# A decoder trunk on one core: the engine that adds the pool projection, and the steps at which four activation sets are fetched

## The chip, the core and the metric

The kernel runs on one core of a Trainium2 chip. A core has five engines that run their own queues of instructions in order: TensorE (PE, matmul, with its weight loads shown as PEld), VectorE (DVE), ScalarE (ACT), GpSimd (POOL) and SyncE (SP), which here issues nearly all DMAs. Engines wait for each other through semaphores. Matmuls write to PSUM banks; everything else lives in SBUF, and the large activations go through device memory between stages.

The metric is the device time of one execution in microseconds.

## What is computed

One layer of a decoder trunk over 2048 positions of width 1024, in float32, cut here to what matters:

```python
u = x * (1 + scale) + shift                      # scale, shift, gate from SiLU(c) @ w_ada
q, k, v, a_gate, p_in, p_gate, m_a, m_p = split(u @ w_in)
a = sliding_window_attention(q, k, v, sinks, bias) * silu(a_gate)
a = a @ w_attn_proj
p = einsum(causal_pool(p_in), w_pool_mix)
p = (p * pool_scale) * silu(p_gate)
p = p @ w_pool_proj
y = sigmoid(m_a) * a + sigmoid(m_p) * p          # the sum that the change touches
y = (y @ w_out) * (1 + gate)
x = layer_norm(ALPHA * x + y)
```

## The kernel before

The 2048 positions are worked in two halves s of 1024, each half in two columns t of 512. Each projection takes two products of matrices into one: a "quad" holds two blocks of 128 output rows (mi = 0, 1) for both columns, and computes its four results with seven products instead of eight, from sums and differences of the weights and of the activations (a scheme of Strassen's kind). The seven products are named B11, T1, T2, B21, T3, B22, T4 after their activation operand. Float32 precision comes from splitting each operand in a rounded part and a remainder, so one product is 4 pieces x 3 = 12 matmuls of 128 x 512.

**The sets.** The seven activation operands of a stage are tiles of their own (`set_B11`, `set_T1`, ...), each of two halves. All quads of a stage use the same seven. At a change of stage, each is fetched from device memory as raw float32 (one DMA of 512 KB for each half, on SP), cast to the rounded part on ScalarE, and its remainder is taken on VectorE (`split` in `set_steps`). A set can be fetched only when the last product of the old stage that reads it is done. Six stages take new sets in this way: the input projections of the second half, then, in the last third of the kernel, attention projection and pool projection of the first half, the same of the second half, and the output projection.

**The order of products.** `ring` runs groups of two quads. A group is 14 steps of one product each: `back` runs T2, B21 of the first quad, T2, B21 of the second (steps 0 to 3), T3, B22, T3, B22 (4 to 7), T4, T4 (8, 9), and then `front` starts the next group with B11, T1, B11, T1 (10 to 13). At the last group of a stage, `front` already belongs to the next stage, and its steps 14 to 27 are the first group of that. `tick` is called behind each product, and runs what is hooked to that step; `defer(n, f)` runs f n steps later. `PLAN` and `SPLIT_AT` name the order and the steps of the casts (B21 at 11 and 12, T3 at 13 and 14, B22 at 15 and 16, T4 at 17 and 18), `FETCH_AT` the steps of the fetches. B21 is first read at step 15, T3 at 18, B22 at 19, T4 at 22.

**The weights.** Each quad loads its weights in three DMAs (L261 to L263; from the sum y, in the output stage, L257). GpSimd makes the sums and differences of them: L268 (`sum1`, needed for T1), L272 and L273 (`mid`), L277 (`late`). ScalarE casts pairs of weight blocks (L305; L312 for the last block) into `w_set`, VectorE takes the remainders (L131). `ask` in `back` has the next quad's weights loaded one step after the current quad's third pair was split, and `sum1` two steps after that.

**Side work.** GpSimd also makes the sums of the next stages' sets: four subtractions on `spare` tiles for each eighth, stored by SP.

**The pool projection.** `pool_quad` takes each of a quad's four results as it is done: VectorE multiplies it by its gate (L610), GpSimd adds it to the attention's share in the `wide` tile (L612), and SP stores the sum to `y_d` three steps later. There are 32 such results, 16 in each half. What a helper (`split_set`, `product`, functions that record their instruction through `Ordered`) issues is shown under L56.

Of the kernel before, what the change touches and what calls it, by code (L numbers as in the profile page):

```python
# [15 lines left out]
ALU = mybir.AluOpType  # L16
# [43 lines left out]
def kernel(  # L60
# [22 lines left out]
    nc = tc.nc  # L83
# [354 lines left out]
    def defer(ticks, f):  # L438
        due.append((now[0] + ticks, len(due), f))
# [48 lines left out]

    SPLIT_AT = (2, 3, 4, 5, 6, 7, 11, 12, 13, 14, 15, 16, 17, 18)

    FETCH_AT = {"B11": -2, "T1": -1, "T2": 3, "B21": 4, "T3": 7, "B22": 8, "T4": 10}

    def set_steps(ph, store):

# [6 lines left out]
        def fetch(name, half):  # L501
            sp.dma_start(raw(name, half), store[name][half])

        def split(name, half):
            t = sets[name][:, 2 * half : 2 * half + 2]
            act.copy(t[:, :, 0, :], raw(name, half))
            low(dve, t[:, :, 1, :], raw(name, half), t[:, :, 0, :])

        for at, (_, name, half) in zip(SPLIT_AT, PLAN):
            todo.append((FETCH_AT[name], lambda n=name, h=half: fetch(n, h)))  # L510
            todo.append((at, lambda n=name, h=half: split(n, h)))
# [70 lines left out]
    def gates_ahead(name, s, m, raw):  # L582
        g = {}

        def ahead(ph, turn):
            for mi, t in (((0, 0), (1, 1)), ((0, 1), (1, 0)))[turn]:
                x = g[mi, t] = ph.c("g")
                sp.dma_start(x, gates_d[name][s, m + mi, t])
                if raw:
                    nc.scalar.activation(x, x, AF.Sigmoid)  # L590

        return g, ahead
# [12 lines left out]
    def pool_quad(s, m):  # L605
        gates, ahead = gates_ahead("mp", s, m, m < 4)

        def consume(ph, mi, t, src):
            g = gates.pop((mi, t))
            nc.vector.tensor_tensor(g, src, g, ALU.mult)  # L610
            dst = ta[m + mi][:, t * CH : (t + 1) * CH]
            nc.gpsimd.tensor_tensor(dst, g, dst, ALU.add)  # L612
            defer(3, lambda: sp.dma_start(y_d[s, m + mi, t], dst))

        return Quad((wpp[m], wpp[m + 1]), consume, ahead)
# [942 lines left out]
```

## Time and profile before

| | us |
|---|---|
| runs, median of 3 (lowest to highest) | 1728.08 (1727.62 to 1729.83) |
| the profiled execution | 1731.03 |
| its span | 1729.2 |
| TensorE busy | 1664.1 |
| VectorE busy | 1254.5 |
| GpSimd busy | 1058.1 |
| ScalarE busy | 964.2 |

The mean clock granted to TensorE in the profiled execution is 0.989 of the full one. By HBM traffic, 227.96 MB are read and 110.33 MB written.

How to read the rows further down. In a timeline: start in us from the span's start, duration in us, engine, source line, operation, output and inputs by the program's names, count; in brackets the idle time of the engine just before, and what ended it. In a list of waits: who waited for whom, total us, times, longest us. In a list of groups: line, engine, operation, shapes, count, then busy us, mean ns, and the idle time before them with its releasers. In a list of DMAs: tiles, queue, kind, count, size, median us from issue to landing. SPq is SyncE's queue.

### The profile page before, as it was taken

What the parts mean: (1) busy time and instruction counts of PE and PEld (TensorE: products, weight loads), DVE (VectorE), ACT (ScalarE), POOL (GpSimd) and SP (SyncE); (2) the same over time, 40 slices, a digit from 0 to 9 for tenths busy, and PEclk for the clock granted to TensorE, in tenths of its full rate; (3) what the DMA queues carried; (4) which work ended last, traced back from release to release, by engine and by line L of the source; (5) the groups of instructions that cost most, each with busy time, mean ns of one, the idle gap of its engine ahead of it and who ended that gap; (6) DMA issues with size and microseconds to landing.
All of it is one profiled execution on the core that took longest, in us unless ns stands there. A gap on an engine that the chain in (4) does not pass through costs nothing.

```text
span 1729.2 us, 24722 instructions
## 1 busy us (share of the span) xinstructions
PE 1664.1 (96%) x8056; PEld 1392.5 (81%) x8056; DVE 1254.5 (73%) x2256; ACT 964.2 (56%) x2002; POOL 1058.1 (61%) x782
## 2 busy tenths in 40 slices
PE   6899999999999999999999999999999989999996
PEld 5788888888888788887788888888787767787885
DVE  5966665787778768557578777786778576868877
ACT  4544446667667655334667676765644345434452
POOL 2054427686867837763476778594657875666442
PEclk9999999999999999999999999999999989999999
DMA  9388753333432377866533434235987887787442
GB/s 353 131 283 287 218 188 111 117 108 122 149 107 95 129 250 277 282 226 207 188 110 104 132 118 153 86 116 185 326 294 275 310 305 272 263 274 239 158 139 105
DMA packets 188849, 336.79 MB, mean 195 GB/s; under 512 B 18336, under 2 KB 44080, under 8 KB 188720
## 3 DMA queue, kind: packets, MB, share of 16 engines
q1 hardware_dynamic: 185600, 330.96, 55.7%
q10 hardware_dynamic: 3088, 4.23, 1.0%
q8 instruction: 64, 1.05, 0.3%
q14 instruction: 65, 0.53, 0.1%
q0 software_dynamic: 32, 0.02, 0.0%
HBM read 227.96 MB, written 110.33 MB: 196 GB/s over the span
## 4 chain that ended last, share of the span: by engine, by line
PE 47%; POOL 7%; DVE 5%; DMA 4%; issue 4%; ACT 1%; SPq 0%; POOLq 0%; DVEq 0%; ACTq 0%
PE mm L56 30%; PE lg L56 13%; PE pv L56 2%; PE pt L56 2%; DVE w_set L131 1%; POOL spare L56 1%; POOL nxt L56 1%; POOL W L268 1%; POOL w_set L56 1%; POOL fin L56 1%; DMA W<-in_wpp_dram 1%; DMA W<-in_wap_dram 1%; DMA pin_T<-spare 1%; POOL wide L612 1%; DVE set_T L56 1%
## 5 line engine op out<-in xcount | busy, mean ns | idle before, releaser
L56 PE MATMUL mm<-set_B,w_set 128*128 128x512 f32 x2664 | 664.8, 397 | 18.3 <-ACT w_set L305 10.5
L56 PEld LDWEIGHTS mm<-set_B,w_set 128*128 128x128 f32 x2664 | 501.2, 190 | 129.1 <-ACT w_set L305 12.6
L56 PE MATMUL mm<-set_T,w_set 128*128 128x512 f32 x1824 | 457.4, 397 | 3.8 <-DVE mm L56 1.2
L56 PE MATMUL lg<-set_T,w_set 128*128 128x512 f32 x1728 | 417.9, 392 | 10.0 <-DVE w_set L131 4.8
L56 PEld LDWEIGHTS mm<-set_T,w_set 128*128 128x128 f32 x1824 | 337.7, 189 | 76.4 <-DVE mm L56 4.1
L56 PEld LDWEIGHTS lg<-set_T,w_set 128*128 128x128 f32 x1728 | 323.9, 189 | 82.7 <-DVE w_set L131 8.4
L131 DVE TENSOR_TENSOR w_set<-W,w_set 128x1024 fp32r<-128x1024 f32 x138 | 198.4, 1439 | 185.9 <-ACT w_set L305 172.8
L305 ACT CAST w_set<-W 128x1024 fp32r<-128x1024 f32 x138 | 144.8, 1050 | 291.0 <-PE mm L56 164.4
L56 POOL TENSOR_TENSOR w_set<-W,w_set 128x512 fp32r<-128x512 f32 x132 | 172.0, 1311 | 102.5 <-ACT w_set L56 98.1
L268 POOL TENSOR_TENSOR W<-W,A 128x512 f32<-128x512 f32 x46 | 70.6, 1535 | 223.8 <-DVE set_T L56 58.2
L56 ACT ACTIVATE L<-L,nm 128x257 f32<-128x257 f32 (+1 forms) x256 | 127.1, 498 | 26.0 <-DVE nm L56 20.2
L56 POOL TENSOR_TENSOR W<-W 128x512 f32<-128x512 f32 x82 | 108.3, 1335 | 51.1 <-DVE sm L56 30.3
L277 POOL TENSOR_TENSOR W<-W 128x512 f32<-128x512 f32 x46 | 72.8, 1583 | 101.6 <-DVE w_set L131 94.0
L56 DVE CUSTOM_DVE_ANT_0 L<-lg,bt,nsink 128x256 f32<-128x256 f32 (+1 forms) x256 | 111.6, 473 | 19.0 <-DMA bt<-e_rep 9.1
L56 POOL TENSOR_TENSOR spare<-spare 128x512 f32<-128x512 f32 x68 | 117.2, 1725 | 12.6 <-DMA spare<-ain_B 8.7
L56 ACT CAST w_set<-W 128x512 fp32r<-128x512 f32 (+1 forms) x164 | 100.0, 626 | 37.4 <-POOL W L56 25.8
L56 DVE COPY o<-pv 64x256 f32<-64x256 f32 x128 | 54.3, 424 | 82.7 <-PE pv L56 81.4
L56 ACT CAST pth<-pt 128x512 fp32r<-128x512 f32 (+1 forms) x128 | 72.8, 569 | 62.8 <-PE pt L56 62.4
L56 ACT ACTIVATE L<-L,sm 128x256 f32<-128x256 f32 (+1 forms) x128 | 64.3, 502 | 67.9 <-DVE sm L56 67.7
L272 POOL TENSOR_TENSOR W<-W 128x512 f32<-128x512 f32 x44 | 75.6, 1720 | 39.1 <-DVE w_set L131 30.1
L273 POOL TENSOR_TENSOR W<-W 128x512 f32<-128x512 f32 x44 | 77.5, 1761 | 28.3 <-DMA W<-in_win_dram 26.6
L56 DVE TENSOR_SCALAR L<-L,sm 128x256 f32<-128x256 f32 (+1 forms) x128 | 89.8, 701 | 0.0
(225 smaller groups left out, 2474.8 us busy)
## 6 DMA issues: line engine op xcount, KB each, us to landing
W<-in_win_dram SPq DMA_DIRECT2D x42, 512.0 KB, 5.5
W<-in_win_dram SPq DMA_DIRECT2D x42, 256.0 KB, 3.7
A<-in_win_dram SPq DMA_DIRECT2D x42, 256.0 KB, 4.7
ag_d<-sig SPq DMA_DIRECT2D x32, 256.0 KB, 5.3
pg_d<-sig SPq DMA_DIRECT2D x32, 256.0 KB, 4.4
pg<-pg_d SPq DMA_DIRECT2D x32, 256.0 KB, 3.3
pin_B<-fin SPq DMA_DIRECT2D x32, 256.0 KB, 2.2
ag<-ag_d SPq DMA_DIRECT2D x32, 256.0 KB, 2.9
```

Source lines behind the costliest of these rows:

```text
L56: return lambda *args, **kw: self.tc.keep_in_program_order(op(*args, **kw))
L131: engine.tensor_tensor(dst, src, as32(hi), ALU.subtract)
L268: e.tensor_tensor(self.w[:, 1, :], self.w[:, 2, :], self.a22, ALU.add)
L272: e.tensor_tensor(x[:, 1, :], x[:, 1, :], x[:, 0, :], ALU.subtract)
L273: e.tensor_tensor(x[:, 2, :], x[:, 0, :], x[:, 2, :], ALU.subtract)
L277: e.tensor_tensor(x[:, 3, :], x[:, 3, :], x[:, 1, :], ALU.subtract)
L305: a.copy(by_two(hi), raw)
L612: nc.gpsimd.tensor_tensor(dst, g, dst, ALU.add)
```

## The change

```diff
-    FETCH_AT = {"B11": -2, "T1": -1, "T2": 3, "B21": 4, "T3": 7, "B22": 8, "T4": 10}
+    FETCH_AT = {"B11": -2, "T1": -1, "T2": 3, "B21": 8, "T3": 10, "B22": 12, "T4": 13}
...
             nc.vector.tensor_tensor(g, src, g, ALU.mult)
             dst = ta[m + mi][:, t * CH : (t + 1) * CH]
-            nc.gpsimd.tensor_tensor(dst, g, dst, ALU.add)
+            nc.vector.tensor_tensor(dst, g, dst, ALU.add)
             defer(3, lambda: sp.dma_start(y_d[s, m + mi, t], dst))
```

Two edits. The fetches of B21, T3, B22 and T4 are put into the program 4, 3, 4 and 3 products later, at each of the six changes of stage; the steps of their casts stay. In the pool projection, the 32 additions to the attention's share run on VectorE, behind the multiplication, instead of on GpSimd. Part of the instructions keep the order in which they are written; the others are placed by a scheduler, so that both edits also change which instruction stands where in the queues of VectorE, ScalarE, GpSimd and SP. TensorE's order stays.

## The prediction

> **What bounds the kernel now.** I read the page first: TensorE is busy 96% of the span.
>
> ```profile
> PE 1664.1 (96%) x8056; PEld 1392.5 (81%) x8056; DVE 1254.5 (73%) x2256; ACT 964.2 (56%) x2002; POOL 1058.1 (61%) x782
> ```
>
> So time can only go where TensorE stands still or runs at less than its full clock. The busy time by stage shows where that is; columns are window, length, busy time of PE, PEld, DVE, ACT, POOL, granted clock, DMA share, GB/s. The windows hold the openings of stages, where seven activation sets are replaced: the second half's projections, then both halves' attention and pool projections, then the output. I call them O0 to O5 (the 1413 row is no opening).
>
> ```profile
> 620.00:700.00 80.00, 80.00 (x355) 66.24 (x354) 58.85 (x50) 43.00 (x57) 47.28 (x28) 1.00 0.85 292
> 1214.00:1240.00 26.00, 23.93 (x97) 19.04 (x96) 15.71 (x13) 15.42 (x21) 17.73 (x10) 0.93 0.90 324
> 1285.00:1323.00 38.00, 36.65 (x160) 29.51 (x159) 32.52 (x29) 24.61 (x35) 24.28 (x14) 1.00 0.98 373
> 1361.00:1413.00 52.00, 42.21 (x161) 31.90 (x161) 35.77 (x32) 22.51 (x26) 41.29 (x25) 0.90 1.00 369
> 1413.00:1475.00 62.00, 60.47 (x267) 49.72 (x266) 47.13 (x43) 31.09 (x42) 36.87 (x23) 1.00 0.75 264
> 1475.00:1495.00 20.00, 17.95 (x71) 14.07 (x70) 13.89 (x12) 9.87 (x13) 15.17 (x9) 0.91 0.88 325
> 1551.00:1589.00 38.00, 35.09 (x146) 27.77 (x145) 35.17 (x30) 15.80 (x18) 28.72 (x16) 0.96 0.75 263
> ```
>
> Idle plus lost clock is 2.1 + 1.8 (0.07 of 26) at O1, 1.35 at O2, 9.8 + 4.0 at O3 (0.10 of 52 is 5.2; part of the slow clock fell on idle time), 1.5 in the 1413 window, 2.05 + 1.8 at O4, 2.9 + 1.5 at O5: 28.8 us. More than that, from these stages, no version of the change can give. O0 has none.
>
> The waits of TensorE from 1214 to 1590 say what ended the idle time: always a weight operand (w_set), its rounded part from ScalarE or its remainder from VectorE.
>
> ```profile
> PE mm L56 <- ACT w_set L305: 10.5, 5, 5.4
> PE mm L56 <- DVE w_set L131: 5.9, 6, 2.0
> PE lg L56 <- DVE w_set L131: 2.8, 4, 1.1
> PE lg L56 <- ACT w_set L305: 0.8, 1, 0.8
> ```
>
> Behind ScalarE stands GpSimd. The timeline at O3:
>
> ```profile
> 1385.67 2.19 POOL L612 TENSOR_TENSOR wide<-g,wide 128x512 f32<-128x512 f32 x1 [1.76 <-DMA pin_T<-spare]
> ...
> 1389.06 1.25 POOL L612 TENSOR_TENSOR wide<-g,wide 128x512 f32<-128x512 f32 x1
> 1390.27 1.25 POOL L268 TENSOR_TENSOR W<-W,A 128x512 f32<-128x512 f32 x1
> ...
> 1391.56 1.04 ACT L305 CAST w_set<-W 128x1024 fp32r<-128x1024 f32 x1 [9.52 <-DMA pin_T<-spare]
> ...
> 1392.66 5.34 PE L56 MATMUL mm<-set_B,w_set 128*128 128x512 f32 x12 [5.39 <-ACT w_set L305]
> ```
>
> The first weight sum of the new stage (L268) stands in GpSimd's queue behind additions (L612) that wait for pool products; the cast and the product follow at once when it ends. The same at O1 (1228.72) and O4 (1481.84), there with other sums of GpSimd ahead of L268:
>
> ```profile
> 1228.72 1.28 POOL L268 TENSOR_TENSOR W<-W,A 128x512 f32<-128x512 f32 x1
> ...
> 1230.04 1.04 ACT L305 CAST w_set<-W 128x1024 fp32r<-128x1024 f32 x1 [5.72 <-POOL W L268]
> ```
>
> ```profile
> 1481.84 1.28 POOL L268 TENSOR_TENSOR W<-W,A 128x512 f32<-128x512 f32 x1
> ...
> 1483.16 1.04 ACT L305 CAST w_set<-W 128x1024 fp32r<-128x1024 f32 x1 [8.66 <-POOL W L268]
> ```
>
> Only O5 is of another kind: the cast was done, VectorE was late, and its queue was full (35.17 of 38 us).
>
> ```profile
> 1558.90 1.69 DVE L131 TENSOR_TENSOR w_set<-W,w_set 128x1024 fp32r<-128x1024 f32 x1
> ...
> 1560.64 1.76 PE L56 MATMUL mm<-set_B,w_set 128*128 128x512 f32 x4 [2.02 <-DVE w_set L131]
> ```
>
> **The additions.** The edit takes 32 additions from GpSimd and gives VectorE the same form. L610 on two SBUF tiles (g from p and g) is the nearest row for the new price, the same from PSUM the lower one:
>
> ```profile
> L612 POOL TENSOR_TENSOR wide<-g,wide 128x512 f32<-128x512 f32 x32 | 56.8, 1780 | 29.0 <-DVE g L610 23.8 <-DMA W<-in_wpp_dram 3.5 <-DMA pin_T<-spare 1.8
> ...
> L610 DVE TENSOR_TENSOR g<-mm,g 128x512 f32<-128x512 f32 x16 | 10.9, 682 | 6.5 <-PE lg L56 3.0 <-DMA g<-mp_d 2.2 <-PE mm L56 1.3
> L610 DVE TENSOR_TENSOR g<-p,g 128x512 f32<-128x512 f32 x8 | 7.8, 973 | 0.2
> ```
>
> GpSimd loses 56.8 us of work and 29.0 us in which its queue stood still for an addition; VectorE gains 32 x 0.68 = 22 to 32 x 0.97 = 31 us. I take 0.8 (26 us), between the two, since GpSimd has less left to collide with. Away from the openings it lies beside products. An addition waits only for the multiplication just ahead of it; queued behind it on VectorE are the weight remainders (L131), and TensorE waits for those, so without cover each costs its 0.8 there. The next row shows the collision:
>
> ```profile
> 1539.41 1.21 DVE L131 TENSOR_TENSOR w_set<-W,w_set 128x1024 fp32r<-128x1024 f32 x1
> 1539.58 2.20 POOL L612 TENSOR_TENSOR wide<-g,wide 128x512 f32<-128x512 f32 x1 [5.44 <-DVE g L610]
> ...
> 1540.55 2.31 DVE L56 TENSOR_TENSOR set_T<-set_T 128x1024 fp32r<-128x1024 f32 x1
> ```
>
> Where an addition overlaps a VectorE split, the split takes 2.31 instead of 1.21 us. So each addition that leaves GpSimd can give VectorE back up to 1.1 us, against the 0.8 it costs. [...]
>
> The store of each sum is queued on SP, which issues in order. From 1214 to 1590 SP stood
>
> ```profile
> SPq L56 <- POOL spare L56: 55.3, 20, 7.5
> SPq L56 <- POOL wide L612: 44.5, 14, 7.0
> ```
>
> so behind those 44.5 us weights, gates and sets were asked for late. With the sum made on VectorE right behind its product, most of that goes.
>
> **The sets.** B21, T3, B22 and T4 are asked for at steps 8, 10, 12, 13 instead of 4, 7, 8, 10, two DMAs of 512 KB each, at each of six openings: 48 of the 84 set transfers. A step is one product:
>
> ```profile
> 1277.34 2.72 PE lg L56 x12
> ```
>
> so the delay is 8.2 to 10.9 us. On SP the next weights now stand ahead of them; the listing of both programs shows SP's queue so, and VectorE and ScalarE with both halves of B21's split behind the second quad's opening operand instead of around it. What that costs is bounded by when a set lands and when its cast stands in ScalarE's queue:
>
> ```profile
> set_B<-u_B SPq DMA_DIRECT2D x6, 512.0 KB, 6.4
> set_B<-wo_B SPq DMA_DIRECT2D x6, 512.0 KB, 7.9
> ```
>
> ```profile
> 642.24 1.38 SPq L56 DMA_DIRECT2D set_B<-u_B  x2
> ...
> 654.73 1.05 ACT L56 CAST set_B<-set_B 128x1024 fp32r<-128x1024 f32 x1
> ...
> 657.76 2.88 PE L56 MATMUL lg<-set_T,w_set 128*128 128x512 f32 x12
> 657.79 1.05 ACT L305 CAST w_set<-W 128x1024 fp32r<-128x1024 f32 x1 [1.52 <-PE mm L56]
> 658.88 1.23 DVE L131 TENSOR_TENSOR w_set<-W,w_set 128x1024 fp32r<-128x1024 f32 x1 [1.59 <-ACT w_set L305]
> ```
>
> B22 at O0, the tightest: asked for 10.9 us later (653.1), landing 6.4 to 7.9 later (659.5 to 661.0), it makes its cast 4.8 to 6.3 us late. Queued behind it on ScalarE is the weight cast of 657.79, whose remainder would end 3.3 to 4.8 us after 660.1, at 663.4 to 664.9; its product is two products after 657.76, at 663.2. So the cost per opening lies between 0.2 and 1.7 us if the landing is no faster, and 0 if SP, no longer held, asks sooner and fewer transfers share the engines. Below 0 lies the gain that the weights land sooner, which I count with the waits. I take 0.5 us at each of six openings, for this and for VectorE's longer queue together: 3 us.
>
> **The sum.** O1: L268 moves ahead of two sums, all 3.9 goes (0 if the weights land too late). O2: 1.35. O3: GpSimd was free at 1383.9 (1385.67 less its idle time); with one sum of 1.25 between, L268 could start at 1385.2, 5 us sooner. Then VectorE ends last, by an estimated 2 us: the stage's eight additions cost it 8 x 0.8 = 6.4, four collisions saved give 4.4. The quoted wait and its slow matmuls (5.34 for 2.72) are 8.0 us, so 6.0 go; of the other 5.8, in smaller waits with mixed causes, I take 2.4, under half. Together 8.4 of 13.8, bounds 3 and 13.8. The 1413 window: nothing, its order is unchanged. O4: 2.8 of 3.85. O5: VectorE is full; five additions ahead of the late operand cost 5 x 0.8 = 4.0, three or four collisions saved give 3.3 to 4.4, so 1.0 of 4.4, bounds -3 and 4.4. Together 3.9 + 1.35 + 8.4 + 2.8 + 1.0 = 17.4; less 3 is 14.4 us. The profiled execution took 1731.0 (span 1729.2), so 1716.6; the median of the runs lies 3.0 lower, 1728.1, so 1713.7, said as 1714.
>
> [...]
>
> **The rivals.**
> *VectorE's queue ends last (17%).* O3, O4 and O5 keep their waits, because the operand now stands behind additions and bunched splits instead of GpSimd's sums. For it: 35.17 of 38 us at O5. Against it: the 1.1 us collisions. Left are O1, O2 and O3's small waits, 7.6 less about 2: 1722.
>
> *Nothing comes of it (9%).* [...] 1728.
>
> *Sets land too late (14%).* ScalarE stops at the cast of a late B22 and the weight cast behind it comes late. It decides where the landing is more than 3.1 us behind the cast's old place (663.2 less 660.1). If SP asks later than its step, at all six openings, with 3.2 us of wait and 1.7 of clock each, 29 us are lost against 17 won: 1740. Against it: before, this set landed some 5 us ahead of its cast (642.24 + 7.9 against 654.73), and TensorE's waits name weights only.
>
> **How the numbers follow.** Forecast 60%: 1714, its own range 1706 to 1722. The four cases give a range of 1704 (24 of the 28.8 us) to 1731, which leaves out most of the last rival and little below. A measurement of this kernel can tell 0.2% (3.5 us) from no change: faster 72% (the forecast and most of the first rival), same 13%, slower 15%.
>
> **What would show it.** Right: no GpSimd row for L612; VectorE rows of 0.7 to 0.9 us; SP's waits for sums down by over 30 us; O1 and O4 without a wait on the L305 cast; clock 1.00 at O1. Wrong: waits of ScalarE's set casts for DMA, or new waits of TensorE for a set; L131 as the only releaser with as much time as now; L268 no earlier against the products.

## The result, and the profile after

The changed kernel takes 1724.2 us in the median of 14 runs (1719.29 to 1726.92), the kernel before, on the same chip, 1728.27 (1726.91 to 1734.14). The ratio is 0.9975, 95% interval 0.9967 to 0.9983: faster by 0.25%, 4.1 us, where 14 were forecast. The profiled executions lie 6.2 us apart (1731.03 and 1724.84).

The page of the kernel after, engines' busy time:

```profile
PE 1659.3 (96%) x8056; PEld 1389.4 (81%) x8056; DVE 1283.1 (74%) x2288; ACT 965.8 (56%) x2002; POOL 1001.9 (58%) x750
```

The work went over as foreseen: GpSimd lost 56.2 us, VectorE gained 28.6. TensorE's waits from 1214 to 1590, after:

```profile
PE mm L56 <- DVE w_set L131: 8.3, 6, 4.9
PE lg L56 <- DVE w_set L131: 7.0, 6, 2.0
PE lg L56 <- ACT w_set L305: 1.8, 2, 1.2
PE lg L56 <- DVE p L389: 1.1, 1, 1.1
```

18.2 us against 20.0 before. The 11.3 us that ended with ScalarE's cast fell to 1.8; the 8.7 us that ended with VectorE's remainder rose to 15.3. So most of the idle time stayed, and its releaser changed. Busy time by stage after, columns as in the prediction:

```profile
1214.00:1240.00 26.00, 24.88 (x108) 19.93 (x108) 14.61 (x13) 15.28 (x22) 18.04 (x11) 1.00 0.88 306
1285.00:1323.00 38.00, 37.17 (x165) 30.45 (x164) 36.80 (x30) 25.13 (x35) 28.13 (x15) 1.00 1.03 391
1361.00:1413.00 52.00, 46.09 (x194) 37.34 (x193) 43.39 (x41) 20.93 (x24) 29.80 (x18) 0.93 1.02 376
...
1475.00:1495.00 20.00, 19.55 (x86) 15.87 (x86) 19.67 (x15) 14.04 (x20) 14.69 (x7) 1.00 0.74 277
1551.00:1589.00 38.00, 37.79 (x160) 30.72 (x159) 36.05 (x37) 17.28 (x21) 13.34 (x9) 0.96 0.83 278
```

At O1 and O4 the granted clock rose to 1.00. At O3 GpSimd's busy time fell from 41.29 to 29.80 of 52 us and VectorE's rose from 35.77 to 43.39; TensorE gained 3.9 us of busy time. The opening of O3 in the timeline after:

```profile
1380.16 1.32 POOL L268 TENSOR_TENSOR W<-W,A 128x512 f32<-128x512 f32 x1 [3.31 <-DMA W<-in_wap_dram]
...
1381.51 1.05 ACT L305 CAST w_set<-W 128x1024 fp32r<-128x1024 f32 x1 [1.79 <-POOL W L268]
1381.94 2.31 DVE L56 TENSOR_TENSOR set_T<-set_T 128x1024 fp32r<-128x1024 f32 x1
...
1386.46 1.18 DVE L612 TENSOR_TENSOR wide<-g,wide 128x512 f32<-128x512 f32 x1
1387.05 1.73 POOL L268 TENSOR_TENSOR W<-W,A 128x512 f32<-128x512 f32 x1
1387.56 2.30 DVE L56 TENSOR_TENSOR set_T<-set_T 128x1024 fp32r<-128x1024 f32 x1
...
1388.74 2.24 POOL L56 TENSOR_TENSOR spare<-spare 128x512 f32<-128x512 f32 x1
...
1389.79 1.75 DVE L612 TENSOR_TENSOR wide<-g,wide 128x512 f32<-128x512 f32 x1
1391.45 0.68 DVE L610 TENSOR_TENSOR g<-lg,g 128x512 f32<-128x512 f32 x1
1392.06 1.21 DVE L131 TENSOR_TENSOR w_set<-W,w_set 128x1024 fp32r<-128x1024 f32 x1
...
1393.32 4.48 PE L56 MATMUL mm<-set_B,w_set 128*128 128x512 f32 x10 [4.86 <-DVE w_set L131]
```

The weight sum starts at 1380.16 instead of 1390.27, and the cast follows at 1381.51. But the remainder of the same weights starts at 1392.06, where it stood before (1392.64). VectorE works without a pause from 1366.40 to here. In its queue stand six additions of 0.69, 0.69, 1.74, 0.68, 1.18 and 1.75 us, 6.73 together. The other 19 instructions of this stretch are the same as before and take some 18.9 us in both. The row of the same remainder before holds what the prediction should have read:

```profile
1392.64 1.23 DVE L131 TENSOR_TENSOR w_set<-W,w_set 128x1024 fp32r<-128x1024 f32 x1 [4.71 <-ACT w_set L305]
```

VectorE had 4.71 us to spare there. After the change it began the stretch 2.57 us sooner (1366.40 instead of 1368.97) and was given 6.73 us more, so the remainder came only 0.58 us sooner.

### The profile page after: what moved, and what is told of

The parts are those of the page before. It is cut to its first block, busy times and chain, and to the rows that moved or that the text cites. A ratio compares the mean times of both kernels' runs of the same rounds, so it can differ in the third digit from the quotient of the medians.

```text
span 1723.1 us, 24716 instructions
## 1 busy us (share of the span) xinstructions
PE 1659.3 (96%) x8056; PEld 1389.4 (81%) x8056; DVE 1283.1 (74%) x2288; ACT 965.8 (56%) x2002; POOL 1001.9 (58%) x750
## 4 chain that ended last, share of the span: by engine, by line
PE 44%; DVE 9%; DMA 6%; POOL 5%; issue 4%; ACT 1%; SPq 0%; POOLq 0%; DVEq 0%; ACTq 0%
PE mm L56 29%; PE lg L56 11%; DVE w_set L131 3%; PE pv L56 2%; PE pt L56 2%; DVE set_T L56 1%; POOL nxt L56 1%; POOL w_set L56 1%; DMA set_T<-ain_T 1%; DMA W<-y_d 1%; DVE set_B L56 1%; DVE wide L612 1%; POOL W L56 1%; POOL fin L56 1%; DMA g<-ma_d 1%
## 5 line engine op out<-in xcount | busy, mean ns | idle before, releaser
L56 PEld LDWEIGHTS lg<-set_T,w_set 128*128 128x128 f32 x1728 | 324.8, 189 | 90.8 <-DVE w_set L131 13.7
L131 DVE TENSOR_TENSOR w_set<-W,w_set 128x1024 fp32r<-128x1024 f32 x138 | 199.4, 1446 | 153.6 <-ACT w_set L305 143.1
L268 POOL TENSOR_TENSOR W<-W,A 128x512 f32<-128x512 f32 x46 | 71.0, 1543 | 252.4 <-ACT w_set L312 58.7
L56 POOL TENSOR_TENSOR W<-W 128x512 f32<-128x512 f32 x82 | 108.4, 1336 | 51.6 <-DVE sm L56 30.3
L56 POOL TENSOR_TENSOR spare<-spare 128x512 f32<-128x512 f32 x68 | 122.4, 1803 | 23.8 <-DMA spare<-pin_B 10.3
L277 POOL TENSOR_TENSOR W<-W 128x512 f32<-128x512 f32 x46 | 69.2, 1504 | 108.8 <-DVE w_set L131 99.7
L272 POOL TENSOR_TENSOR W<-W 128x512 f32<-128x512 f32 x44 | 72.2, 1645 | 68.7 <-DVE w_set L131 59.7
L273 POOL TENSOR_TENSOR W<-W 128x512 f32<-128x512 f32 x44 | 79.3, 1803 | 30.7 <-DMA W<-in_win_dram 27.9
```

Of the source, the lines that this page charges most:

```text
L56: return lambda *args, **kw: self.tc.keep_in_program_order(op(*args, **kw))
L131: engine.tensor_tensor(dst, src, as32(hi), ALU.subtract)
L268: e.tensor_tensor(self.w[:, 1, :], self.w[:, 2, :], self.a22, ALU.add)
L272: e.tensor_tensor(x[:, 1, :], x[:, 1, :], x[:, 0, :], ALU.subtract)
L273: e.tensor_tensor(x[:, 2, :], x[:, 0, :], x[:, 2, :], ALU.subtract)
L277: e.tensor_tensor(x[:, 3, :], x[:, 3, :], x[:, 1, :], ALU.subtract)
```

## The experiments

Each run is compared with the kernel before on the same chip. Its median on the four chips was 1730.8 (e1 to e4), 1730.4 (e5 to e8), 1731.4 (e9 to e11), 1729.7 (e12 to e15) and 1728.4 (e16, e17), so the ratios compare better than the times. The expectations give times as on the chip of the result, where the kernel before takes 1728.3; there, a run's time is its ratio times this.

| run | median us | ratio to before (95%) |
|---|---|---|
| the whole change | 1724.2 | 0.9975 (0.9967 to 0.9983) |
| e1 additions only | 1726.0 | 0.9971 (0.9959 to 0.9983) |
| e2 fetches only | 1726.5 | 0.9977 (0.9966 to 0.9988) |
| e3 no additions, late fetches | 1712.4 | 0.9896 (0.9880 to 0.9912) |
| e4 no additions, old fetches | 1712.5 | 0.9900 (0.9885 to 0.9916) |
| e5 store does not wait | 1723.4 | 0.9964 (0.9950 to 0.9978) |
| e6 no additions of m = 4, 6 | 1715.3 | 0.9907 (0.9886 to 0.9928) |
| e7 additions 2 later | 1727.1 | 0.9977 (0.9964 to 0.9989) |
| e8 half on each engine | 1721.9 | 0.9947 (0.9929 to 0.9966) |
| e9 T2 splits later | 1725.2 | 0.9964 (0.9950 to 0.9979) |
| e10 half on each, T2 later | 1725.8 | 0.9967 (0.9952 to 0.9981) |
| e11 before, T2 later | 1734.4 | 1.0017 (1.0006 to 1.0029) |
| e12 no side sums | 1708.2 | 0.9879 (0.9861 to 0.9897) |
| e13 side sums later | 1723.3 | 0.9964 (0.9949 to 0.9978) |
| e14 before, side sums later | 1732.2 | 1.0012 (1.0000 to 1.0024) |
| e15 half on each, side sums later | 1725.4 | 0.9976 (0.9962 to 0.9989) |
| e16 products in PSUM | 1720.2 | 0.9949 (0.9935 to 0.9962) |
| e17 products in PSUM, side sums later | 1717.6 | 0.9937 (0.9924 to 0.9949) |

**Which edit, and what the additions cost at all.** e1 puts the old fetch steps back into the whole change, e2 puts the additions back on GpSimd.

```diff
-    FETCH_AT = {"B11": -2, "T1": -1, "T2": 3, "B21": 8, "T3": 10, "B22": 12, "T4": 13}
+    FETCH_AT = {"B11": -2, "T1": -1, "T2": 3, "B21": 4, "T3": 7, "B22": 8, "T4": 10}
```

> The additions on VectorE, the four sets fetched at their old steps. Theory Q (VectorE's queue took GpSimd's place at the openings, the moved fetches matter little): within 2 us of the whole change, about 1724, waits of TensorE on L131 near 15 us from 1214 to 1590. Theory B (the moved fetches bunch the set splits ahead of weight remainders and give back what the additions won): 1719 or less, the new waits at 1236 to 1252 gone.

```diff
-            nc.vector.tensor_tensor(dst, g, dst, ALU.add)
+            nc.gpsimd.tensor_tensor(dst, g, dst, ALU.add)
```

> The four sets fetched later, the additions still on GpSimd. Theory Q: the cast waits behind GpSimd's first weight sum come back, 1726 to 1729, near the kernel before. Theory B: slower than before by 3 us or more, 1731 to 1734, with L131 as releaser at the first attention opening.

e3 leaves the line of the addition out of the whole change, e4 out of the kernel before.

```diff
-            nc.vector.tensor_tensor(dst, g, dst, ALU.add)
```

> The 32 additions are left out of the changed kernel (so the pool projection's share is missing from y); everything else as in it. Theory Q: without its 26 us of additions VectorE keeps up, 1710 to 1714, the waits at the second half's opening and at the output's opening mostly gone. Theory B: no faster than 1720, since the bunched splits stay.

> The 32 additions are left out, the sets fetched at their old steps (the pool projection's share is missing from y). Theory Q: 1710 to 1714, as with the late fetches. Theory B: at least 4 us below the run without additions and with late fetches.

Each edit alone gives what both give, 0.23 to 0.29%, so the gains don't add. Theory B's times failed in all four runs. Q's came in e1, e3 and e4; e2 is a little faster than Q had it (1724.3 by its ratio), and there Q's reason failed: TensorE's waits for the cast did not come back (2.8 us from 1214 to 1590, 11.3 before), and 13.7 us end with L131 though no addition runs on VectorE. With the fetches alone, the scheduler puts the weight sum at O3 ahead of an addition:

```profile
1383.17 2.28 POOL L268 TENSOR_TENSOR W<-W,A 128x512 f32<-128x512 f32 x1
1385.49 1.05 ACT L305 CAST w_set<-W 128x1024 fp32r<-128x1024 f32 x1 [3.43 <-POOL W L268]
1386.09 2.18 POOL L612 TENSOR_TENSOR wide<-g,wide 128x512 f32<-128x512 f32 x1 [0.63 <-DVE g L610]
...
1389.41 4.08 PE L56 MATMUL mm<-set_B,w_set 128*128 128x512 f32 x10 [2.08 <-DVE w_set L131]
...
1396.72 1.05 ACT L305 CAST w_set<-W 128x1024 fp32r<-128x1024 f32 x1 [10.18 <-POOL W L268]
...
1397.82 0.73 PE L56 MATMUL mm<-set_B,w_set 128*128 128x512 f32 x2 [1.60 <-ACT w_set L305]
```

The first operand's wait fell from 5.39 to 2.08 us, with VectorE as its releaser, and the second operand still waits for GpSimd. With the additions alone (e1) it is the other way round. The second operand does not wait, and the first waits for VectorE, longer than before:

```profile
1398.43 4.41 PE L56 MATMUL mm<-set_B,w_set 128*128 128x512 f32 x10 [5.91 <-DVE w_set L131]
```

The whole change has the picture of e1: what the fetches win at the first operand is lost when the additions stand on VectorE.

Without additions the time is 1712.4 and 1712.5 us: by the ratios they cost 1.0% (17 us) on GpSimd in the kernel before (e4), and 0.8% (0.9975 less 0.9896, 14 us) on VectorE in the changed one (e3). The forecast of 1714 would have needed additions that cost some 4 us in all (0.9917 less 0.9896). With them gone, the fetch steps make no difference.

**Whether it is the store, the place or the group.** e5 stores the product instead of the sum, e6 leaves half of the additions out, e7 moves them, e8 divides them.

```diff
-            defer(3, lambda: sp.dma_start(y_d[s, m + mi, t], dst))
+            defer(3, lambda: sp.dma_start(y_d[s, m + mi, t], g))
```

> The whole change, but SP stores the gated pool product g to y_d instead of the sum; the additions still run on VectorE, and no store waits for them (the attention's share is missing from what is stored). Theory S: the additions cost because SP, which issues in order, stands at their stores and asks for weights and sets late; then the price goes with the wait, and the time comes near the versions without additions, 1712 to 1716 us. Theory Q: they cost because they stand in VectorE's queue ahead of the first weight remainder of the next stage; then nothing changes, 1721 to 1727 us, and the wait for a remainder at the opening of the second half's attention projection (4.9 us in the whole change's trace) stays over 3 us.

```diff
-            nc.vector.tensor_tensor(dst, g, dst, ALU.add)
+            if m < 4:
+                nc.vector.tensor_tensor(dst, g, dst, ALU.add)
```

> The whole change with the 16 additions of the quads m = 4 and 6 left out in both halves (the pool's share is missing from those blocks); the 16 of m = 0 and 2 run on VectorE. The last group of a stage is made of m = 4 and 6, so these are the ones that stand at an opening. Theory Q (queue at the opening): nearly the whole price of the additions goes with them, 1711 to 1716 us. [...]

```diff
-            nc.vector.tensor_tensor(dst, g, dst, ALU.add)
-            defer(3, lambda: sp.dma_start(y_d[s, m + mi, t], dst))
+            defer(2, lambda: nc.vector.tensor_tensor(dst, g, dst, ALU.add))
+            defer(5, lambda: sp.dma_start(y_d[s, m + mi, t], dst))
```

> The whole change with each addition put 2 products later on VectorE, and its store 5 instead of 3 products behind the product. Theory Q: the listing of VectorE's queue has the same additions ahead of the first remainder of the new stage at the second half's attention projection, in another order, so the 4.9 us wait stays and the time is 1720 to 1727 us. Rival M (it is the single place behind the multiplication that costs): 1713 to 1718 us. Theory S expects slower, 1726 to 1732 us, since stores come later still.

```diff
-            nc.vector.tensor_tensor(dst, g, dst, ALU.add)
+            e = nc.gpsimd if mi != t else nc.vector
+            e.tensor_tensor(dst, g, dst, ALU.add)
```

> The whole change, but two of each quad's four additions, (mi, t) = (0, 1) and (1, 0), run on GpSimd, the other two on VectorE. Theory Q: at the opening each of the two queues has half the additions ahead of its part of the first weight operand; VectorE loses some 5 us of the work ahead of the remainder, GpSimd gains 2 additions of 1.8 us ahead of the weight sum, which had 4 to 9 us to spare behind VectorE; the wait falls under 2 us and the time is 1714 to 1720 us, faster than either whole. [...]

Theory S fell with e5: no store waits for an addition any more, SP's waits at these stores fell from 44.8 to 28.1 us, and the time is that of the whole change within the intervals. In e6 most of the price went (0.68 of 0.79%) with the 16 additions of the last groups, as Q expected; there the remainder at O3 starts 0.03 us after the end of its cast and TensorE does not wait:

```profile
1384.59 2.17 POOL L268 TENSOR_TENSOR W<-W,A 128x512 f32<-128x512 f32 x1 [4.04 <-DMA W<-in_wap_dram]
1386.80 1.05 ACT L305 CAST w_set<-W 128x1024 fp32r<-128x1024 f32 x1 [3.08 <-POOL W L268]
1387.88 1.23 DVE L131 TENSOR_TENSOR w_set<-W,w_set 128x1024 fp32r<-128x1024 f32 x1 [1.67 <-ACT w_set L305]
```

e7 is no better than the whole change, so the single place behind the multiplication is not it. Its wait at O3, which Q had left at 4.9 us, is 6.49. e8 came out 0.28% under the whole change, its interval just beneath. By its ratio that is Q's time (1719 us), but not for Q's reason: the wait at O3, which Q had under 2 us, is 4.06 in its trace.

**Whether another load in VectorE's queue would do as well.** If all that counts is what stands ahead of the remainder at O3, then moving two set splits behind it must help as much as moving additions. e9 does so in the whole change, e10 with e8's division besides, e11 in the kernel before. Rival A, that the additions cost by themselves, since VectorE has the same work, had 1722 to 1727 us for e9.

```diff
-    SPLIT_AT = (2, 3, 4, 5, 6, 7, 11, 12, 13, 14, 15, 16, 17, 18)
+    SPLIT_AT = (2, 3, 4, 5, 10, 11, 11, 12, 13, 14, 15, 16, 17, 18)
```

> The whole change, additions on VectorE as they are, but the casts and remainders of the set T2 stand at steps 10 and 11 instead of 6 and 7 (T2 is first read at step 14): on VectorE the two T2 remainders (2.3 us each in the whole change's trace) go behind the first weight remainder of the new stage. Theory Q (the queue ahead of that remainder costs, whatever is in it): at the second half's attention projection the wait of 4.9 us falls under 1.5 us and the time is 1714 to 1720 us, with the additions still in. [...]

> The last one with half the additions (results (0, 1) and (1, 0)) on GpSimd. Theory Q: both queues are short ahead of the first weight operand; 1711 to 1717 us, at or under the one with all of them on VectorE, and near the versions without additions. Rival A: as with half on each, 1719 to 1724 us.

> The kernel before, with only the T2 casts at steps 10 and 11: additions on GpSimd, fetches at their old steps. Theory Q: there VectorE waited for the cast, and the cast for GpSimd's weight sum behind the additions; so the edit that helps the changed kernel gives little here, 1725 to 1731 us, and the wait for the L305 cast at the second half's attention projection stays over 3 us. Rival B (the T2 splits cost by themselves, whichever engine adds): 6 to 10 us faster than before here as well, 1718 to 1723 us.

Q's numbers for e9 and e10 failed; e9 lies in A's range, and so does e10 by its ratio (1722.5; the 1725.8 measured on its chip is above both). The wait did fall, but another took its place one operand later. TensorE's waits at O3 in e9:

```profile
1397.88 4.14 PE L56 MATMUL mm<-set_B,w_set 128*128 128x512 f32 x10 [2.08 <-DVE w_set L131]
1399.13 2.26 POOL L268 TENSOR_TENSOR W<-W,A 128x512 f32<-128x512 f32 x1
1401.42 1.05 ACT L305 CAST w_set<-W 128x1024 fp32r<-128x1024 f32 x1 [7.41 <-POOL W L268]
...
1405.80 1.21 DVE L131 TENSOR_TENSOR w_set<-W,w_set 128x1024 fp32r<-128x1024 f32 x1
1407.07 3.35 PE L56 MATMUL mm<-set_B,w_set 128*128 128x512 f32 x9 [1.85 <-DVE w_set L131]
```

2.08 + 1.85 us stand where 4.86 stood, and the time is that of the whole change within the intervals. The kernel before became 0.17% slower by the same edit (e11), where Q had expected little gain and B much. This suggests that what is short at O3 is not one place in a queue but the time of VectorE and GpSimd together over some 40 us; no run shows that by itself.

**What makes the additions dear.** Theory P: GpSimd's work beside them, here its side sums, keeps them at 1.06 us in the mean, where half of them take 0.69 or less. e12 leaves the side sums out, e13 and e14 move those of the last five eighths (20 of the 48), with their loads and stores, away from O3 (in the whole change, in the kernel before), e15 adds e8's division. Theory P had for e12 0.7 to 0.85 us an addition, a wait at O3 under 1 us and 1708 to 1716 us in all, for e15 1716 to 1723 us.

```diff
-                todo.append((at, sub(out, a, c)))
+                if ph.name != "mix":
+                    todo.append((at, sub(out, a, c)))
```

> The whole change with the 48 side subtractions of GpSimd in the last third (spare<-spare) left out; their loads and stores stay (so the sums T1, T2, T3 and T4 of the later stages' sets are missing), and all additions run on VectorE. [...] Theory K (their number in VectorE's queue costs, each by its own 0.69): the wait stays at 2 to 4 us and the time at 1718 to 1724 us.

```diff
-                at = int(2 + 8 * n + offset)
+                at = int(2 + 8 * n + 10 * (n > 6) + offset)
```

> The whole change, complete, with the side sums of the last five eighths 10 products later, so that none of them stands in the last group of the first half's pool projection. Theory P: the wait of 4.9 us falls under 2 us, some of it comes back where the sums go: 1714 to 1721 us. Theory K: 1721 to 1727 us.

> The kernel before with the same shift of the side sums. There they stand on GpSimd ahead of the weight sum (L268) that is late, two of them in the last 10 us. Theory P: this wait shrinks by 2 to 4 us, the additions beside the splits remain on GpSimd: 1723 to 1729 us. Theory K (only GpSimd's queue counts there): the same or a little better, 1722 to 1726 us; this run does not tell them apart, it says whether the shift needs the change.

> Half of the additions on each engine, as before, and the side sums of the last five eighths 10 products later. [...] Theory K: both queues are shorter, 1712 to 1718 us.

e12's time is on P's side: with every addition still on VectorE it is the fastest run, 1708.2 us. The price of an addition fell less than P said, to 0.92 us; the line is shifted by one:

```profile
L613 DVE TENSOR_TENSOR wide<-g,wide 128x512 f32<-128x512 f32 x32 | 29.3, 915 | 0.7
```

The wait at O3 fell to 1.85 us, between the theories. The 84 set splits took 124.9 us, 15.8 less than in the whole change, so there is more in this run than the price of the additions; GpSimd's own queue became free too. Moving the side sums instead (e13) takes most of the wait at O3 away, but waits appear where they go (2.09 us at 1508), and the median is 1723.3, K's side; e14 and e15 came out above what either theory had given.

**The operand's place alone.** VectorE's L610 from a PSUM bank took 0.67 to 0.69 us in every row before. e16 writes three of four products back to their bank, so that 24 additions read one operand from PSUM; number, engine and order stay. e17 moves the side sums as well. Theory P had for e16 0.68 to 0.72 us for each of the 24, waits at the openings shorter by half or more, and 1714 to 1720 us.

```diff
             g = gates.pop((mi, t))
-            nc.vector.tensor_tensor(g, src, g, ALU.mult)
+            x = g if mi == t == 1 else src
+            nc.vector.tensor_tensor(x, src, g, ALU.mult)
             dst = ta[m + mi][:, t * CH : (t + 1) * CH]
-            nc.vector.tensor_tensor(dst, g, dst, ALU.add)
+            nc.vector.tensor_tensor(dst, x, dst, ALU.add)
```

> The whole change, complete, but three of each quad's four gated pool products are written back to their PSUM bank instead of to the gate's tile, so that 24 of the 32 additions read one operand from PSUM (as L610 does, 0.68 us in every row) and one from SBUF; the eight of results (1, 1) stay on two SBUF tiles. The number and order of VectorE's instructions stay. [...] Theory K (their number in the queue): at most 24 x 0.38 = 9 us less VectorE work, of which the openings see a third: 1720 to 1726 us.

> The last one with the side sums of the last five eighths 10 products later. Theory P: 1712 to 1719 us, no more than 3 us better than without the shift, since the additions no longer meet the side sums. Theory K: as with the shift alone, 1720 to 1725 us.

The additions in e16, as groups; the first row has both operands in SBUF:

```profile
L613 DVE TENSOR_TENSOR wide<-g,wide 128x512 f32<-128x512 f32 x8 | 11.8, 1481 | 0.2
...
L613 DVE TENSOR_TENSOR wide<-mm,wide 128x512 f32<-128x512 f32 x16 | 11.0, 687 | 0.3
...
L613 DVE TENSOR_TENSOR wide<-lg,wide 128x512 f32<-128x512 f32 x8 | 5.5, 682 | 0.1
```

The 24 take 0.69 us in the mean, the other eight 1.48 in the same execution. The time fell 0.26% under the whole change (the intervals do not touch), to the border between P and K; but P's sign failed: in the profiled execution the longest wait at O3 is still 4.91 us, and TensorE's waits from 1214 to 1590 are 19.1 us against 18.2, where P had halved them. e17 gives 1717.6 us, 2.6 us better than e16, as P had it, though the two intervals overlap: 0.63% under the kernel before and 0.38% under the whole change, by its median the fastest version that leaves nothing out. How the price of the additions divides between GpSimd's work beside them and the number of instructions ahead of a remainder is left open.

## Why the prediction was too high, point by point

**What bounds, and where it could come from: right.** All of the gain lies at the openings named, and the releaser at O1, O3 and O4 was GpSimd's weight sum behind ScalarE's cast: those waits fell from 11.3 to 1.8 us. Of its own signs, GpSimd has no addition left, O4 has no wait on the cast (O1 still has one, of 0.59 us), and the clock at O1 is 1.00. The rows of the additions and SP's waits are not as foretold, and the sign named for the other case appeared: L131 as nearly the only releaser.

**Term by term.** TensorE runs the same 8056 matmuls in the same order in all these executions, so the start of the same product can be compared, and each stretch between two such starts has its own gain, the time by which it became shorter. Around the wait that the prediction quotes, the product ahead of it starts at 1378.95 before and 1378.35 after, and the one behind it here:

```profile
1397.83 2.43 PE L56 MATMUL mm<-set_T,w_set 128*128 128x512 f32 x10
1397.64 2.70 PE L56 MATMUL mm<-set_T,w_set 128*128 128x512 f32 x11
```

The lead of 0.6 us shrank to 0.2: this wait gave nothing. The gains of all stretches, in us, of one profiled execution each (times of the kernel before):

| stretch | forecast | whole change | without additions (e3) |
|---|---|---|---|
| up to 1227 | 0 | -0.9 | -0.4 |
| O1, 1227 to 1261 | 3.9 | -0.5 | -0.2 |
| O2, 1261 to 1320 | 1.35 | 1.0 | 0.4 |
| 1320 to 1356 | 0 | -3.2 | 0.3 |
| O3, the quoted wait, 1379 to 1398 | 6.0 | -0.4 | 8.0 |
| O3, its other waits, 1356 to 1379 and 1398 to 1407 | 2.4 | 8.1 | 7.5 |
| O4, 1407 to 1506 | 2.8 | 1.8 | 1.5 |
| O5, 1506 to 1596 | 1.0 | 0.2 | 4.6 |
| sets, at six openings | -3.0 | in the rows | in the rows |
| together | 14.4 | 6.1 | 21.7 |

Three steps failed: the quoted wait at O3, O1 with its new sets, and the stretch between O2 and O3. That O3 as a whole came near its forecast (7.7 of 8.4) is luck: the gain came from the waits of which the prediction took under half, not from the one that it worked out. With the additions alone (e1) these other waits go too, with the fetches alone (e2) they stay. Each of the three is taken up below.

**The first step that failed** is in the sum, at O3: "Then VectorE ends last, by an estimated 2 us: the stage's eight additions cost it 8 x 0.8 = 6.4, four collisions saved give 4.4." Both terms were wrong. The price: 1.06 us in the mean, over the upper bound of 0.97, 9.2 us for the eight between 1367 and 1396, and 6.73 for the six ahead of the remainder. The collisions: none was saved there. Of the five set splits of that stretch, two were longer than 1.22 us before (2.31 and 1.71), and two after (2.31 and 2.30). The groups after:

```profile
L56 DVE TENSOR_TENSOR set_T<-set_T 128x1024 fp32r<-128x1024 f32 x48 | 75.5, 1579 | 6.8 <-ACT set_T L56 6.8
...
L56 DVE TENSOR_TENSOR set_B<-set_B 128x1024 fp32r<-128x1024 f32 x36 | 65.2, 1829 | 4.4 <-ACT set_B L56 4.4
...
L612 DVE TENSOR_TENSOR wide<-g,wide 128x512 f32<-128x512 f32 x32 | 33.8, 1057 | 0.7
```

and the same splits before:

```profile
L56 DVE TENSOR_TENSOR set_T<-set_T 128x1024 fp32r<-128x1024 f32 x48 | 77.3, 1611 | 4.6 <-ACT set_T L56 4.6
...
L56 DVE TENSOR_TENSOR set_B<-set_B 128x1024 fp32r<-128x1024 f32 x36 | 66.8, 1859 | 1.7 <-ACT set_B L56 1.6
```

Over the whole kernel the 84 set splits became 3.4 us shorter. The two edits work against each other here: the splits took 144.1 us before, 133.7 in e1, 148.5 in e2 and 140.7 in the whole change. So moving the 32 additions shortened them by 8 to 10 us, 0.2 to 0.3 for each addition and not 1.1, and the later fetches lengthened them by 4 to 7. At O3 GpSimd's next instructions moved up into the time that the additions left, and met the same splits: in the timeline above, L268 and a side sum lie beside the split of 1387.56, which still takes 2.30. So VectorE got 6.73 us more ahead of a remainder for which it had 4.71. Without the additions the quoted wait gives 8.0 us (e3). This is the prediction's first rival, "VectorE's queue ends last", at O3 and O5; its 1722 us is near by chance, since it counted on the gain at O1 and left O4 its wait.

**O5** gave 0.2 of 1.0. A wait as long as before stands at another product, behind an addition of 1.66 us and a split of 2.31, and the clock falls again (0.96):

```profile
1546.13 2.31 DVE L56 TENSOR_TENSOR set_T<-set_T 128x1024 fp32r<-128x1024 f32 x1
...
1549.69 3.88 PE L56 MATMUL lg<-set_T,w_set 128*128 128x512 f32 x11 [2.00 <-DVE w_set L131]
```

Without the additions it gives 4.6.

**Between O2 and O3**, where nothing was expected, 3.2 us were lost, the second step that failed. There are three new waits (0.69, 1.18 and 0.40 us), which the execution without additions (e3) does not have, so "away from the openings it lies beside products" did not hold in the pool projection's own first group. With the additions alone (e1) the same stretch loses 2.6 us:

```profile
1335.73 2.57 PE L56 MATMUL lg<-set_T,w_set 128*128 128x512 f32 x10 [0.69 <-DVE w_set L131]
...
1344.92 1.39 PE L56 MATMUL lg<-set_T,w_set 128*128 128x512 f32 x5 [1.18 <-ACT w_set L305]
```

**The sets** were the third: 0.5 us at each opening. At O1 the old waits of 1.54 and 0.53 us and the slow matmuls behind them went, and 3.5 us of new waits took more than their place. The timeline at O1 after:

```profile
1236.56 0.73 PE L56 MATMUL lg<-set_T,w_set 128*128 128x512 f32 x2 [0.59 <-ACT w_set L305]
...
1237.82 2.58 PE L56 MATMUL lg<-set_T,w_set 128*128 128x512 f32 x10 [0.52 <-DVE w_set L131]
...
1238.48 3.98 DVE L56 TENSOR_TENSOR set_T<-set_T 128x1024 fp32r<-128x1024 f32 x2 [0.72 <-ACT set_T L56]
...
1242.38 2.32 DVE L131 TENSOR_TENSOR w_set<-W,w_set 128x1024 fp32r<-128x1024 f32 x1
...
1244.75 2.58 PE L56 MATMUL lg<-set_T,w_set 128*128 128x512 f32 x10 [1.19 <-DVE w_set L131]
...
1245.22 4.16 DVE L56 TENSOR_TENSOR set_B<-set_B 128x1024 fp32r<-128x1024 f32 x2
...
1251.67 1.66 PE L56 MATMUL lg<-set_T,w_set 128*128 128x512 f32 x6 [1.16 <-DVE w_set L131]
```

Both halves of a split now stand together, 4 us at once, and the remainder behind them comes 1.2 us late, twice. The mechanism was the one named (splits bunched in VectorE's queue), not a late landing: TensorE never waits for a set (the list of its waits names none), so the rival "sets land too late" did not occur. No run shows the 3.2 us of wait and 1.7 us of lost clock that its 1740 puts at each opening for a late set: the new waits there were 0.52 to 1.19 us at O1, for weights, with a clock of 1.00. At O0, for which the 0.5 was worked out, the cast of B22 starts 3.0 us later (657.69) and no product waits for what stands behind it. Both, the gain and the new waits, come from the fetches: e2 has them, and e1 keeps the old wait of 1.54 us for the cast, since no addition stands in GpSimd's queue there.

**SP's waits**: the step that said that most of the 44.5 us would go was wrong, though nothing hung on it. After:

```profile
SPq L56 <- DVE wide L612: 44.8, 21, 5.0
```

SP waits for the result whichever engine makes it. In e5 the waits at the stores were 17 us less and the time was the same, so they do not set it.

## What to carry to other kernels

Before work is moved to another engine, read that engine's idle time just ahead of the operand that is late: that row (4.71 us) bounds what it can take, whatever the first engine gains. Don't book the end of a collision in full: the engine that is relieved goes on with its next instruction, and in a full stage that collides too (here 0.2 to 0.3 us came back for each addition, where 1.1 was booked). Check a forecast stretch by stretch: a total that is near can hide a term that gave nothing. Where two engines are short together, take work away, or give an instruction an operand in PSUM (here 0.69 us, against 1.48 with both in SBUF); rearranging moved the wait to the next operand (2.08 and 1.85 us for 4.86 in e9).

## What the runs showed of the hardware

With one operand in PSUM, no VectorE addition was lengthened by GpSimd's work: 0.68 to 0.69 us in each of 24 (e16), against 1.48 in the mean of eight with both operands in SBUF in the same execution. One of the 24, at 1387.79, took 0.68 us wholly beside GpSimd's L268 (1386.75 to 1388.99). Moving the additions alone gave 0.29% (e1), leaving them out 1.0% (e4).

The length of the waits alone did not decide how fast TensorE went on. At O1 before, 1.54 and 0.53 us of idle time within 2 us went with a clock of 0.93 over 26 us, and the ten matmuls behind them took 3.83 us; in e1, behind the same two waits, 1.54 and 0.52 us, the same ten took 2.56 us. After, waits of 0.59, 0.52, 1.19 and 1.16 us over 16 us went with a clock of 1.00; at O5 after, a wait of 2.00 us, which ended at 1549.69, stood ahead of a clock of 0.72 from 1550 to 1556, 0.96 over the 38 us from 1551. What decides between equal waits, no run here shows.

One execution is not the median. The whole change ran between 1719.3 and 1726.9 us; e13's profiled execution has a span of 1715.9 us, where its median stands for 1721.5 (1723.3 less the 1.8 us around a span). Single waits of 1 to 2 us in one trace are not a verdict.
